# A hybrid decoder layer on one core: another order of the first products, the last tile's squares and root by blocks of 128 tokens, sums rounded in halves, one scaling by VectorE

## The chip, the core and the metric

The kernel runs on one core of a Trainium2 chip. The metric is the device time of one execution in microseconds (us); a run's time is that of its only core. Three runs of the kernel before took 1079.01, 1079.30 and 1079.93 us, median 1079.3. Each profile is of one more execution.

The core has five engines, each with its own queue of instructions, which it works through in order: TensorE (PE in the profile; its weight loads are PEld), VectorE (DVE), ScalarE (ACT), GpSimd (POOL) and SyncE (SP), which here only issues transfers. An instruction waits on semaphores for the instructions of other engines whose results or buffers it needs.

## What is computed

One inference layer over 576 tokens (a prompt of 512 and eight samples of 8), model width 1024:

```python
u = _rms(x) * g_pre_mix
proj = u @ w_in                       # split into the parts of two recurrences
...
mix = jnp.concatenate([y_ssd, h_ml], axis=-1) @ w_out
x = x + _rms(mix) * g_post_mix
u = _rms(x) * g_pre_x                 # cross-attention over 256 memory positions
...
o = jnp.einsum('bhlm,bmhd->blhd', pr, mem_v).reshape(bsz, length, X_WIDTH) @ w_xo
x = x + _rms(o) * g_post_x
u = _rms(x) * g_pre_ffn
f = (jax.nn.silu(u @ w_gate) * (u @ w_up)) @ w_down
x = x + _rms(f) * g_post_ffn
```

with `_rms(x) = x * rsqrt(mean(x * x) + eps)` per token. All in 32-bit floats; the kernel also returns the states of the recurrences and the memory's keys and values.

## The kernel before

**Products.** Every factor is kept as two tensors of a shorter format: a rounded part (`hi`: `whi`, `uh`, `hh`, `wdh`) and the remainder (`lo`: `wlo`, `ul`, `hl`, `wdl`). A cast, mostly by ScalarE, makes the rounded part; a subtraction, mostly by VectorE, makes the remainder (`split`, `split_w`). One product of a 128-row piece is then three matmuls into one PSUM bank: hi with hi, hi with lo, lo with hi (`gemm`, L201 to L212). The eight pieces of a 1024-long sum run one after the other. Features lie on the 128 partitions and tokens along the columns. The tokens go in two halves: 256 and 320 columns (`HALVES`) in the input projection and at the end, 288 and 288 (`EHALVES`) in between.

**Who sets the order.** Most of the program is handed to a planner, which orders the instructions of each engine by a simulated timeline, starting from the order of the program text; `tc.issue_after(i)` makes the instructions of its block follow `i` in the queue of their engine. The stretches under `tc.manual_schedule` (the middle of the kernel, and the end from L2302) run in an order written out by hand: `at_(p, fn)` puts a function at a place `p`, one unit being the products of one tile, and the sorted list is issued as it stands. Operations on one PSUM bank are kept in order as a whole.

**The start (L303 to L352).** `NWARM` products on zeros run on TensorE while the first transfers are under way. x arrives piece by piece (`xraw`, one piece of 128 features for each k; the first in two token halves), and two weight tiles (`raws`) arrive in four parts of two pieces each. ScalarE scales x into its rounded part (L333), VectorE makes the remainder (L334); the weights' parts are cast and subtracted behind them (L339, through L197 and L198; the very first cast is VectorE's, L330). TensorE takes, for each k and each of the two weight tiles, both token halves, three matmuls each (L350 to L352).

**The cross-attention's output (`xo`, from L1539).** Eight tiles of 128 features for the first 288 tokens. When a tile's products are done, ScalarE squares the bank (L270, L274 in `add_sq`) and scales it into `f` (L1560). For tiles 0 to 2 both are kept back until tile 3 begins (`kept_back`). Tile j takes a bank that tile j - 3 has given up, and its products are put behind `evx[j - 3]`, the last reading of that bank.

**The feed-forward part (from L1828).** `Pair` (gate and up projection) and `Down` (down projection) make two output tiles at once from seven products of combined factors instead of eight (`Seven`). For this, sums and differences of weights are made on VectorE (`sums`, into `sw`, the second half LB first, then LA) and split again (`parts2`: cast at L197, subtraction at L198). In `early` of a `Down` the order of the products is 0, 1, 3, 2; product 3 uses LB of the sum's parts, product 2 uses LA. Four `Down` groups run in each of two stages, beside the pairs.

**The last down projection (L2158 to L2173 and the list that follows).** It adds the last six of 22 pieces. Weights of tiles 0 to 4 go to `wdh` and `wdl` (cast and subtraction of 768 columns), those of tiles 5 to 7 to the usual buffers. The order for the second half of the tokens is tile 6, 7, 0, 1, 2, 3, 4, 5; the first three run their first four pieces before the last hidden values (`hh`, `hl`), which come from the last gate and up pair (`done`, L1935, then `put`), are there.

**The end (L2178 to L2304).** The 256 tokens of the first half go tile by tile (`half0`): the bank is added to `f2` (L2214), squared (L2217), scaled by the gain (L2219, for tile 7 by VectorE, L2221), and the squares are summed (L2224). For tile 7 the squares go straight into the sums over the features, products with ones (`root`, L2186), one column per block of 128 tokens. From these VectorE and ScalarE make the reciprocal root (L2190 to L2199; both blocks at once, as two columns). TensorE meanwhile turns `x` and `f2` into token rows (`x_rows`, `f_rows`); at the end VectorE adds root times rows to x for three of the four parts (`last`, L2270), ScalarE scales the fourth (`scaled`, L2280), VectorE adds it (`scaled_add`, L2283), and each part is stored.

Of the kernel before, what the change touches and what calls it, by code (L numbers as in the profile page):

```python
# [11 lines left out]
F32 = mybir.dt.float32  # L12
# [97 lines left out]
NWARM = 19  # L110
# [5 lines left out]
def build(nc, tc, ctx, I, O):  # L116
# [53 lines left out]
    loads, casts, accs = [], [], []  # L170
# [7 lines left out]
    def split_w(src, n=1024, cut=CUT, acc=False, pool=None, to=None, raw=None):  # L178
# [3 lines left out]
        if to:  # L182
            split(*to, raw[:, :n])
            return to
# [83 lines left out]
    def add_sq(pool, ssq, src, j, w=T, eng=None, t0=0, q=None):  # L268
        if j == 0:
            A.activation(ssq[:, t0:t0 + w], src, AF.Square)  # L270
# [45 lines left out]
    for k in range(KT):  # L316
# [11 lines left out]

        if k == 0:
            V.tensor_copy(wi[0][0][:, c], raws[0][:, c])  # L330
        for t0, n in ([(0, T)] if k else HALVES):
            ts_ = slice(t0, t0 + n)
            uhk = A.activation(uh[:, k, ts_], xraw[:, k, ts_], AF.Copy, scale=PAR("g_pre", k))  # L333
            ulk = V.scalar_tensor_tensor(ul[:, k, ts_], xraw[:, k, ts_], PAR("g_pre", k), uh[:, k, ts_].bitcast(F32),  # L334
                                         op0=ALU.mult, op1=ALU.subtract)
        if k % 2 == 0:
            for i in range(2):
                with tc.issue_after(uhk.ins), tc.issue_after(ulk.ins):
                    split(wi[i][0][:, c], wi[i][1][:, c], raws[i][:, c], cast=None if k or i else lambda *_: None)  # L339
# [5 lines left out]
    for k in range(KT):  # L345
        for (hi, lo), pss in zip(wi, ps0):
            wh, wl = hi[:, k * P:(k + 1) * P], lo[:, k * P:(k + 1) * P]
            for (t0, n), ps in zip(HALVES, pss):
                ah, al = U(k, t0, n), UL(k, t0, n)
                mm(ps, wh, ah, start=k == 0, stop=False)  # L350
                mm(ps, wh, al, start=False, stop=False)
                mm(ps, wl, ah, start=False, stop=k == KT - 1)  # L352
# [1186 lines left out]
    def xo(j, i, pool=None):  # L1539
# [11 lines left out]
        def step(k0, k1):  # L1551
# [5 lines left out]

            def out():
                add_sq(ph, ssq, ps, j if i == 0 else XO1.index(j), n, t0=t0)
                evx[at_e] = A.activation(f[:, j, t0:t0 + n], ps, AF.Copy, scale=PAR("g_postx", j))  # L1560
# [267 lines left out]
    class Seven:  # L1828
# [85 lines left out]
    class Pair(Seven):  # L1914
# [8 lines left out]
        def done(s, a, i, ps, more=None):  # L1923
# [11 lines left out]
            V.tensor_tensor(g, g, ps, op=ALU.mult)  # L1935
# [198 lines left out]
    class Plain:  # L2134
# [3 lines left out]
        def put(s, j, a, i, g):  # L2138
            split(*[t_[:, j % 8, E[i]] for t_ in s.b], g)
# [41 lines left out]
    def root(name, terms, chunks):  # L2181
# [5 lines left out]
        v, y, a, r = few[:] if n == 3 else [fp.tile([P, n], F32, name=name + k) for k in ("_v", "_y", "_a", "_r")]  # L2187
        w = fp.tile([P, n], F32, name=name + "_w")
        tail[name], tail["w", name] = (w, y, a, r), w
        V.tensor_scalar(v, ps[:, :n], 1.0 / 1024.0, EPS, op0=ALU.mult, op1=ALU.add)  # L2190
        A.activation(y, v, AF.Sqrt)
        V.reciprocal(tail["w", name], v)

    def root_end(name):
# [5 lines left out]
        tail[name] = r  # L2200
# [67 lines left out]
    def last(i):  # L2268
        o, rc = xt[i][0], tail["pf0"][:, parts[i][0]:parts[i][0] + 1]
# [8 lines left out]
    def scaled():  # L2278
        tail["s"] = sw[:, 0:512].rearrange("p (j k) -> p j k", j=4)
        A.activation(tail["s"], ft[3], AF.Copy, scale=tail["pf0"][:, parts[3][0]:parts[3][0] + 1])  # L2280

    def scaled_add():
        V.tensor_tensor(xt[3][0], xt[3][0], tail["s"], op=ALU.add)  # L2283
# [134 lines left out]
```

## Time and profile before

| | |
|---|---|
| median of three runs | 1079.3 us |
| the profiled execution | 1077.81 us |
| its span, first to last instruction | 1075.9 us |
| mean granted TensorE clock | 0.997 |
| busy: TensorE products, weight loads | 1066.2 us (99%), 1013.8 us (94%) |
| busy: VectorE, ScalarE, GpSimd | 751.8 us (70%), 607.6 us (56%), 231.7 us (22%) |
| matmuls | 8122 |
| last matmul ends, last VectorE operation ends, span ends | 1068.96, 1072.45, 1075.9 us |

Times in rows count from the first instruction. A matmul is pipelined: its recorded duration (0.28 to 0.31 us for 256 to 320 columns) is over twice the distance to the next one's start, so TensorE's share of busy time says little; the distance between starts says whether it waited.

### The profile page before, as it was taken

What the parts mean: (1) busy time and instruction counts of PE and PEld (TensorE: products, weight loads), DVE (VectorE), ACT (ScalarE), POOL (GpSimd) and SP (SyncE); (2) the same over time, 40 slices, a digit from 0 to 9 for tenths busy, and PEclk for the clock granted to TensorE, in tenths of its full rate; (3) what the DMA queues carried; (4) which work ended last, traced back from release to release, by engine and by line L of the source; (5) the groups of instructions that cost most, each with busy time, mean ns of one, the idle gap of its engine ahead of it and who ended that gap; (6) DMA issues with size and microseconds to landing.
All of it is one profiled execution on the core that took longest, in us unless ns stands there. A gap on an engine that the chain in (4) does not pass through costs nothing.

```text
span 1075.9 us, 20705 instructions
## 1 busy us (share of the span) xinstructions
PE 1066.2 (99%) x8122; PEld 1013.8 (94%) x8122; DVE 751.8 (70%) x1509; ACT 607.6 (56%) x1094; POOL 231.7 (22%) x305
## 2 busy tenths in 40 slices
PE   9999999999999999999999999999999999999997
PEld 8999887778999999999999989999999999999997
DVE  6897775758877775559655555766467887787556
ACT  7778522345654556556555445545566566656653
POOL 1454543213213111000154201100011111111000
PEclk9999999999999999999999999999999999999998
DMA  6785544435655349643468775743476687578532
GB/s 208 177 161 131 157 138 166 147 85 172 197 148 150 107 131 341 234 168 116 143 212 286 266 256 171 252 127 94 133 180 142 156 201 165 116 190 185 128 132 89
DMA packets 58966, 181.76 MB, mean 169 GB/s; under 512 B 6604, under 2 KB 12108, under 8 KB 58356
## 3 DMA queue, kind: packets, MB, share of 16 engines
q1 hardware_dynamic: 42884, 138.22, 38.4%
q0 software_dynamic: 15408, 41.43, 19.3%
q8 instruction: 64, 1.05, 0.4%
q10 hardware_dynamic: 576, 0.79, 0.2%
q14 instruction: 34, 0.28, 0.1%
HBM read 159.75 MB, written 20.65 MB: 168 GB/s over the span
## 4 chain that ended last, share of the span: by engine, by line
PE 95%; DVE 3%; ACT 1%; issue 1%; DMA 0%; SPq 0%; DVEq 0%; ACTq 0%
PE ps_in L208 6%; PE ps_in L211 6%; PE ps_in L209 6%; PE ps_v L854 5%; PE ps_o L211 3%; PE ps_g L1910 3%; PE ps_g L1909 3%; PE ps_o L209 3%; PE ps_g L1911 3%; PE ps_o L208 3%; PE ps_u L1910 3%; PE ps_u L1911 3%; PE ps_u L1909 3%; PE ps_dn L1909 2%; PE ps_dn L1910 2%; PE ps_dn L1911 2%
## 5 line engine op out<-in xcount | busy, mean ns | idle before, releaser
L208 PE MATMUL ps_in<-uh,whi 128*128 128x320 f32 (+1 forms) x544 | 161.7, 297 | 0.0
L211 PE MATMUL ps_in<-uh,wlo 128*128 128x320 f32 (+1 forms) x544 | 161.7, 298 | 0.0
L209 PE MATMUL ps_in<-ul,whi 128*128 128x320 f32 (+1 forms) x544 | 161.0, 296 | 0.0
L186 ACT CAST whi<-raw 128x1024 fp32r<-128x1024 f32 (+1 forms) x104 | 105.3, 1014 | 94.3 <-PE ps_in L209 27.7
L193 DVE TENSOR_TENSOR wlo<-raw,whi 128x1024 fp32r<-128x1024 f32 (+2 forms) x97 | 94.7, 978 | 59.6 <-ACT whi L186 58.7
L211 PEld LDWEIGHTS ps_in<-uh,wlo 128*128 128x128 f32 x544 | 102.1, 188 | 2.0 <-issue 1.3
L208 PEld LDWEIGHTS ps_in<-uh,whi 128*128 128x128 f32 x544 | 102.3, 188 | 1.7 <-issue 0.8
L209 PEld LDWEIGHTS ps_in<-ul,whi 128*128 128x128 f32 x544 | 102.3, 188 | 0.4
L191 POOL DMA_DIRECT2D wlo<-win x31 | 27.0, 872 | 78.0 <-ACT wlo L190 65.5
L1909 PE MATMUL ps_g<-b,whi 128*128 128x288 f32 x144 | 42.5, 295 | 0.0
L1910 PE MATMUL ps_g<-b,whi 128*128 128x288 f32 x144 | 42.4, 295 | 0.0
L1910 PE MATMUL ps_u<-b,whi 128*128 128x288 f32 x144 | 42.2, 294 | 0.0
L1909 PE MATMUL ps_u<-b,whi 128*128 128x288 f32 x144 | 42.2, 294 | 0.0
L1882 ACT CAST whi<-rawx 128x1024 fp32r<-128x1024 f32 (+1 forms) x26 | 25.7, 988 | 27.6 <-PE ps_dn L1910 13.7
L198 DVE TENSOR_TENSOR wlo<-sw,whi 128x1024 fp32r<-128x1024 f32 (+1 forms) x26 | 29.6, 1140 | 15.0 <-ACT whi L197 14.9
L208 PE MATMUL ps_xo<-qh,whi 128*128 128x288 f32 x128 | 38.4, 302 | 0.1
L209 PE MATMUL ps_xo<-ql,whi 128*128 128x288 f32 x128 | 37.7, 296 | 0.0
L211 PE MATMUL ps_o<-mixm_h,wlo 128*128 128x256 f32 (+1 forms) x128 | 37.7, 295 | 0.0
L209 PE MATMUL ps_o<-mixm_l,whi 128*128 128x256 f32 (+1 forms) x128 | 37.5, 293 | 0.0
L211 PE MATMUL ps_xq<-u2h,wlo 128*128 128x320 f32 (+1 forms) x128 | 37.5, 294 | 0.0
L211 PE MATMUL ps_o<-mixs_h,wlo 128*128 128x320 f32 (+1 forms) x128 | 37.4, 292 | 0.0
L209 PE MATMUL ps_xq<-u2l,whi 128*128 128x320 f32 (+1 forms) x128 | 37.4, 294 | 0.0
(770 smaller groups left out, 3842.2 us busy)
## 6 DMA issues: line engine op xcount, KB each, us to landing
raw<-win SPq DMA_DIRECT2D x35, 512.0 KB, 4.2
raw<-wout SPq DMA_DIRECT2D x17, 512.0 KB, 4.4
raw<-wxq SPq DMA_DIRECT2D x13, 512.0 KB, 3.9
raw<-wgate SPq DMA_DIRECT2D x13, 512.0 KB, 3.5
raw<-wup SPq DMA_DIRECT2D x13, 512.0 KB, 4.8
wlo<-win POOLq DMA_DIRECT2D x24, 256.0 KB, 5.1
kva<-vc SPq DMA_DIRECT2D x11, 512.0 KB, 6.6
raw<-wv SPq DMA_DIRECT2D x10, 512.0 KB, 4.3
```

Of the source, the lines that this page charges most:

```text
L186: casts.append(A.copy(hi[:, :n], raw[:, :n]))
L191: accs.append(G.dma_start(lo[:, a:b], src[:, a:b], accum_op=ALU.add))
L193: e.tensor_tensor(lo[:, a:b], raw[:, a:b], hi[:, a:b].bitcast(F32), op=ALU.subtract)
L198: (eng or V).tensor_tensor(lo, src, hi.bitcast(F32), op=ALU.subtract)
L208: mm(ps, wh, ah, start=i == 0, stop=False)
L209: mm(ps, wh, al, start=False, stop=False)
L211: m = mm(ps, tiles[order[c]][1], xh(order[c], t0, n), start=False, stop=c == len(tiles) - 1)
L854: mm(ps, a, b, skip_group_check=True, **kw)
L1882: A.copy(s.h3[:, s.all], s.r2[:, s.all])
L1909: mm(ps, wh, b[0][k], start=start and k == 0, stop=False, skip_group_check=True)
L1910: mm(ps, wh, b[1][k], start=False, stop=False, skip_group_check=True)
L1911: m = mm(ps, wl, b[0][k], start=False, stop=k == nk - 1, skip_group_check=True)
```

## The change

Four edits. The first piece's products are taken for both weight tiles in the first token half before the second half, with the operations that feed them in that order, and the warm-up has 17 products instead of 19. The cross-attention's tile 0 is scaled by VectorE when its products end. The down groups' sums are cast in two halves, LB first. At the end: tile 0's weight remainder in two pieces, some operations put behind others in their queues (tile 2's weights before tile 1's), tile 7's addition and squares by blocks of 128 tokens, block 0's root as before but for one column, block 1's root by five operations on GpSimd, and the last addition shared between GpSimd and VectorE.

```diff
-NWARM = 19
+NWARM = 17
...
         if to:
-            split(*to, raw[:, :n])
+            with tc.issue_after(after.ins) if after else ExitStack():
+                A.copy(to[0], raw[:, :n])
+            with tc.issue_after(behind.ins) if behind else ExitStack():
+                for a in range(0, n, piece or n):
+                    b = a + (piece or n)
+                    wlows.append(V.tensor_tensor(to[1][:, a:b], raw[:, a:b], to[0][:, a:b].bitcast(F32), op=ALU.subtract))
             return to
...
+        def x_parts(t0, n):
+            ts_ = slice(t0, t0 + n)
+            return (A.activation(uh[:, k, ts_], xraw[:, k, ts_], AF.Copy, scale=PAR("g_pre", k)),
+                    V.scalar_tensor_tensor(ul[:, k, ts_], xraw[:, k, ts_], PAR("g_pre", k), uh[:, k, ts_].bitcast(F32),
+                                           op0=ALU.mult, op1=ALU.subtract))
+
+        def w_parts(i):
+            hi, lo, raw = wi[i][0][:, c], wi[i][1][:, c], raws[i][:, c]
+            h = (A.copy if k or i else V.tensor_copy)(hi, raw)
+            return h, V.tensor_tensor(lo, raw, hi.bitcast(F32), op=ALU.subtract)
+
         if k == 0:
             V.tensor_copy(wi[0][0][:, c], raws[0][:, c])
-        for t0, n in ([(0, T)] if k else HALVES):
...
-        if k % 2 == 0:
-            for i in range(2):
+            x_parts(*HALVES[0])
+            V.tensor_tensor(wi[0][1][:, c], raws[0][:, c], wi[0][0][:, c].bitcast(F32), op=ALU.subtract)
+            h, l = w_parts(1)
+            with tc.issue_after(h.ins), tc.issue_after(l.ins):
+                uhk, ulk = x_parts(*HALVES[1])
+        else:
+            uhk, ulk = x_parts(0, T)
+            if k % 2 == 0:
                 with tc.issue_after(uhk.ins), tc.issue_after(ulk.ins):
-                    split(wi[i][0][:, c], wi[i][1][:, c], raws[i][:, c], cast=None if k or i else lambda *_: None)
+                    w_parts(0)
+                    w_parts(1)
...
     for k in range(KT):
-        for (hi, lo), pss in zip(wi, ps0):
+        for i, h in ((0, 0), (1, 0), (0, 1), (1, 1)) if k == 0 else ((0, 0), (0, 1), (1, 0), (1, 1)):
+            (hi, lo), (t0, n), ps = wi[i], HALVES[h], ps0[i][h]
             wh, wl = hi[:, k * P:(k + 1) * P], lo[:, k * P:(k + 1) * P]
-            for (t0, n), ps in zip(HALVES, pss):
-                ah, al = U(k, t0, n), UL(k, t0, n)
+            ah, al = U(k, t0, n), UL(k, t0, n)
+            with tc.issue_after(first.ins) if k == 0 and h else ExitStack():
                 mm(ps, wh, ah, start=k == 0, stop=False)
                 mm(ps, wh, al, start=False, stop=False)
-                mm(ps, wl, ah, start=False, stop=k == KT - 1)
+                m = mm(ps, wl, ah, start=False, stop=k == KT - 1)
+            if k == 0 and h == 0:
+                first = m
...
+            if (j, i) == (0, 0):
+                V.tensor_scalar(f[:, j, t0:t0 + n], ps, PAR("g_postx", j), None, op0=ALU.mult)
+
             def out():
-                add_sq(ph, ssq, ps, j if i == 0 else XO1.index(j), n, t0=t0)
-                evx[at_e] = A.activation(f[:, j, t0:t0 + n], ps, AF.Copy, scale=PAR("g_postx", j))
+                e = add_sq(ph, ssq, ps, j if i == 0 else XO1.index(j), n, t0=t0)
+                evx[at_e] = e if (j, i) == (0, 0) else A.activation(f[:, j, t0:t0 + n], ps, AF.Copy, scale=PAR("g_postx", j))
...
         def parts2(s):
...
-            split(s.h2[:, s.all], s.l2[:, s.all], sw[:, s.all])
+            for c in (s.LB, s.LA) if isinstance(s, Down) else [s.all]:
+                A.copy(s.h2[:, c], sw[:, c])
+            V.tensor_tensor(s.l2[:, s.all], sw[:, s.all], s.h2[:, s.all].bitcast(F32), op=ALU.subtract)
...
-            V.tensor_tensor(g, g, ps, op=ALU.mult)
+            s.product = V.tensor_tensor(g, g, ps, op=ALU.mult)
...
-            split(*[t_[:, j % 8, E[i]] for t_ in s.b], g)
+            s.cast = split(*[t_[:, j % 8, E[i]] for t_ in s.b], g)
...
         if j not in kept:
+            behind = {}
+            if j == 2:
+                behind[2] = last.product
+            if j == 1:
+                w_of(2)
+                behind[1] = wlows[-1]
...
-            kept[j] = split_w(src, 768, 768, raw=raw, to=None if j > 4 else (wdh[:, j, :], wdl[:, j, :]))
+            kept[j] = split_w(src, 768, 768, raw=raw, to=None if j > 4 else (wdh[:, j, :], wdl[:, j, :]),
+                              piece=384 if j == 0 else None, behind=behind.get(j), after=stores[-1].cast if j == 3 else None)
...
-        v, y, a, r = few[:] if n == 3 else [fp.tile([P, n], F32, name=name + k) for k in ("_v", "_y", "_a", "_r")]
+        v, y, a, r = [t_[:, 0:(3, 1)[n == 2]] for t_ in few]
...
-        V.tensor_scalar(v, ps[:, :n], 1.0 / 1024.0, EPS, op0=ALU.mult, op1=ALU.add)
+        V.tensor_scalar(v, ps[:, :v.shape[-1]], 1.0 / 1024.0, EPS, op0=ALU.mult, op1=ALU.add)
         A.activation(y, v, AF.Sqrt)
-        V.reciprocal(tail["w", name], v)
+        V.reciprocal(w, v)
+        if n == 2:
+            v, y, a, r = [fp.tile([P, 1], F32, name=name + k) for k in ("_v1", "_y1", "_a1", "_r1")]
+            V.tensor_scalar(v, ps[:, 1:2], 1.0 / 1024.0, EPS, op0=ALU.mult, op1=ALU.add)
+            G.tensor_tensor(y, v, C32("nhalf")[:, :1], op=ALU.pow)
+            G.tensor_tensor(a, y, y, op=ALU.mult)
+            G.tensor_tensor(a, a, v, op=ALU.mult)
+            G.tensor_scalar(a, a, -0.5, 1.5, op0=ALU.mult, op1=ALU.add)
+            G.tensor_tensor(r, a, y, op=ALU.mult)
+            tail["r", 1] = r
...
-        V.tensor_tensor(fj, fj, tail[j], op=ALU.add)
...
-        A.activation(squares[j] if j else ssqf[:, 0:256], fj, AF.Square)
+        o = squares[j] if j else ssqf[:, 0:256]
+        for c in [slice(0, 256)] if j < 7 else [slice(0, P), slice(P, 256)]:
+            V.tensor_tensor(fj[:, c], fj[:, c], tail[j][:, c], op=ALU.add)
+            A.activation(o[:, c], fj[:, c], AF.Square)
...
-        o, rc = xt[i][0], tail["pf0"][:, parts[i][0]:parts[i][0] + 1]
+        o, rc = xt[i][0], tail["r", parts[i][0]]
...
-        A.activation(tail["s"], ft[3], AF.Copy, scale=tail["pf0"][:, parts[3][0]:parts[3][0] + 1])
+        A.activation(tail["s"], ft[3], AF.Copy, scale=tail["r", 1])
...
-        V.tensor_tensor(xt[3][0], xt[3][0], tail["s"], op=ALU.add)
+        for e, j in ((G, slice(0, 2)), (V, slice(2, 4))):
+            e.tensor_tensor(xt[3][0][:, j], xt[3][0][:, j], tail["s"][:, j], op=ALU.add)
```

More of the change, by code (lines that the diff above doesn't have):

```diff
@@ L167, in build @@
     ident, ones = C32("ident"), C32("ones")
-    loads, casts, accs = [], [], []
+    loads, casts, accs, wlows = [], [], [], []
     def hi_lo(pool=None):
@@ L176, in hi_lo, with split_w @@
         return hi, (pool or wp).tile([P, 1024], F32R, name="wlo", tag="wlo", bufs=NWX if pool else 3)
-    def split_w(src, n=1024, cut=CUT, acc=False, pool=None, to=None, raw=None):
+    def split_w(src, n=1024, cut=CUT, acc=False, pool=None, to=None, raw=None, piece=None, behind=None, after=None):
         if raw is None:
@@ L269, in add_sq @@
         if j == 0:
-            A.activation(ssq[:, t0:t0 + w], src, AF.Square)
+            return A.activation(ssq[:, t0:t0 + w], src, AF.Square)
         else:
@@ L2199, in root_end @@
         V.scalar_tensor_tensor(r, r, 1.5, a, op0=ALU.add, op1=ALU.mult)
-        tail[name] = r
+        tail[name] = tail["r", 0] = r
     def root_rows1():
```

8 lines of the change are left out of this document (2 added, 6 removed).

## The prediction

> **What bounds the kernel now.** I read the chain of waits first, then TensorE's own waits, then the order of time around each place that the diff touches.
>
> ```profile
> PE 95%; DVE 3%; ACT 1%; issue 1%; DMA 0%; SPq 0%; DVEq 0%; ACTq 0%
> ...
> PE ps_warm L309 <- DVE wz L306: 1.1, 1, 1.1
> PE ps_in L350 <- ACT uh L333: 0.8, 1, 0.8
> PE ps_yi L682 <- DVE lm L675: 0.3, 1, 0.3
> PE ps_ct L589 <- ACT r L567: 0.2, 1, 0.2
> ```
>
> The first row is the chain that ended last, by engine: TensorE (PE) is 95% of it. The others are all the waits of TensorE that this view counts (who <- for whom: us, times, longest). No part of the change removes a counted product (two of the 19 warm-up products fall away, in front of the first stall), so a gain can only be a wait of TensorE that goes, or time before its first or after its last product. The view is short by some waits: a matmul's end is modelled and overlaps the next one, so a late start of under 0.15 us does not count as idle. Those are read from start to start in the order of time, below.
>
> **The start.** Order of time; columns are start, duration, engine, line, operation, and in brackets the idle time before it.
>
> ```profile
> 1.06 4.24 PE L309 MATMUL ps_warm<-wz 128*128 128x256 bf16 x19 [1.06 <-DVE wz L306]
> ...
> 5.25 0.28 PE L351 MATMUL ps_in<-ul,whi 128*128 128x256 f32 x1
> 6.37 0.68 PE L350 MATMUL ps_in<-uh,whi 128*128 128x320 f32 x2 [0.84 <-ACT uh L333]
> 9.56 0.69 PE L350 MATMUL ps_in<-uh,whi 128*128 128x256 f32 x4
> ...
> 5.75 0.56 ACT L333 ACTIVATE uh<-xraw,par 128x320 fp32r<-128x320 f32 x1 [1.81 <-DMA xraw<-xT]
> 8.68 0.70 ACT L197 CAST whi<-raw 128x256 fp32r<-128x256 f32 x2
> ```
>
> TensorE ran two products of the first piece, then stood from 5.25 to 6.37, because the second token half of x lands only for the 5.75 row. The change puts the six products of the first half (two weight tiles, three products each) ahead. What they need besides is made earlier: the second tile's rounding on ScalarE goes ahead of the 5.75 row into 1.81 us of idle time, and both tiles' remainders on VectorE ahead of the second half's. So four more 256-column products run inside the stall. Starts of 288-column products lie 0.13 us apart (rows of the next part), so 256 columns take 0.13 x 256/288 = 0.115 us, and four 0.46. The cap is the next weights: the piece that begins at 9.56 needs the two casts of the 8.68 row, the first of them done at about 9.07 and paced by transfers that the change doesn't move, so TensorE can begin it at 9.12 at best, 0.44 us earlier. I take **0.40**; the bounds are 0 (the new order only makes TensorE wait at 9.1 instead) and 0.46. The two warm-up products (4.24 us for 19, 0.21 us between starts) end 0.43 us earlier, all of it in front of the stall: worth nothing by itself, and nothing lost as long as the first product's weights, which were ready before the warm-up ended, stay so.
>
> **The first cross-attention output tile, one scaling by VectorE.**
>
> ```profile
> 634.21 0.41 ACT L270 ACTIVATE ssqxo<-ps_xo 128x288 f32<-128x288 f32 x1
> 634.51 0.49 ACT L1560 ACTIVATE f_xo<-ps_xo,par 128x288 f32<-128x288 f32 x1
> ...
> 634.50 0.30 PE L209 MATMUL ps_xo<-ql,whi 128*128 128x288 f32 x1
> 634.64 0.29 PE L211 MATMUL ps_xo<-qh,wlo 128*128 128x288 f32 x1
> 635.06 0.40 PE L208 MATMUL ps_xo<-qh,whi 128*128 128x288 f32 x1
> 635.29 0.30 PE L209 MATMUL ps_xo<-ql,whi 128*128 128x288 f32 x1
> ```
>
> Starts of 288-column products lie 0.13 us apart (0.14 in the first pair shown). From 634.64 to 635.06 it is 0.42, so 0.29 was waited, for the bank that L1560 releases at 635.00. The next interval, 0.23, is 0.10 over the normal one: a restart costs that too, since the weight load is no longer hidden. With the scaling on VectorE the bank is released by the square, at 634.62, ahead of 634.77 when TensorE wants it. The whole **0.39** goes. The new VectorE operation (about 0.45 us, an estimate from the 288-column addition at 1029.89 below) is issued when the tile's products end, several us earlier, off the chain; were it late, it could cost at most its own length there.
>
> **The down projection's sums rounded in halves.**
>
> ```profile
> 840.46 0.52 ACT L197 CAST u3h<-d 128x384 fp32r<-128x384 f32 x1
> 842.38 0.84 ACT L197 CAST whi<-sw 128x768 fp32r<-128x768 f32 x1 [0.65 <-PE ps_dn L1910]
> ...
> 842.92 0.29 PE L1911 MATMUL ps_dn<-te,wlo 128*128 128x288 f32 x1
> 843.27 0.41 PE L1909 MATMUL ps_dn<-hh,whi 128*128 128x288 f32 x1
> ...
> 942.90 0.29 PE L1911 MATMUL ps_dn<-te,wlo 128*128 128x288 f32 x1
> 943.24 0.41 PE L1909 MATMUL ps_dn<-hh,whi 128*128 128x288 f32 x1
> ```
>
> In both down stages TensorE waits once for the 768-column rounding: 0.35 and 0.34 from start to start, 0.21 over normal, and 0.10 of restart each. The product that waits is the one on the second half (LB), and that half is now rounded first: 384 columns take 0.52, so it is ready at 842.90 instead of 843.22, before 843.05 when TensorE is free. Both waits go: **0.62**. Two casts for one cost ScalarE about 0.2 us (2 x 0.52 against 0.84) in each of the eight groups; ScalarE is on 1% of the chain, so I count nothing, and 0 to -0.2 us per stage as the other bound, if the second half is then late.
>
> **The last down projection's weights.**
>
> ```profile
> 1027.78 0.96 DVE L198 TENSOR_TENSOR wdl<-raw,wdh 128x768 fp32r<-128x768 f32 x1 [0.41 <-ACT wdh L197]
> 1029.03 0.95 DVE L198 TENSOR_TENSOR wdl<-rawx,wdh 128x768 fp32r<-128x768 f32 x1
> 1029.89 0.45 DVE L1935 TENSOR_TENSOR gt<-gt,ct 128x288 f32<-128x288 f32 x1
> ...
> 1028.30 0.31 PE L208 MATMUL ps_dn<-hh,wdh 128*128 128x320 f32 x1
> 1028.45 0.31 PE L209 MATMUL ps_dn<-hl,wdh 128*128 128x320 f32 x1
> 1028.80 0.41 PE L211 MATMUL ps_dn<-hh,wdl 128*128 128x320 f32 x1
> ...
> 1030.50 0.30 PE L209 MATMUL ps_dn<-hl,wdh 128*128 128x320 f32 x1
> 1030.86 0.56 PE L208 MATMUL ps_dn<-hh,whi 128*128 128x320 f32 x2
> ```
>
> Two waits again. At 1028.80 (0.35 against 0.15) TensorE waits for tile 0's remainder, in one piece from 1027.78 to 1028.74; as two pieces of 384 the first is ready at about 1028.33, before 1028.60. At 1030.86 (0.36) it waits for the last hidden values, whose product (L1935, 1029.89) stood behind tile 1's remainder (1029.03). With that remainder put behind the product and behind tile 2's, the product can start 0.8 us earlier. With restarts that is 0.30 + 0.31 = **0.61**. What is late next: tile 1's remainder now ends near 1031.4 instead of 1029.97, and behind it on VectorE stand the hidden values' own remainders; TensorE has other tiles' first terms to run meanwhile, so I take the full 0.61 but keep 0 as the lower bound. On SyncE's queue the two loads change places; tile 5's load, which takes tile 1's buffer, goes about 1.4 us later with it, and that tile is the last in the order.
>
> **The tail.** TensorE's last sums, then the root, three scaled additions (L2270), the last addition (L2283) and the store; rows of POOL in groups of equal operation and shape (busy, mean ns).
>
> ```profile
> 1068.09 0.61 PE L2186 MATMUL ps_ss<-c,sq 128*128 128x1 f32 x4
> 1068.73 0.16 DVE L2190 TENSOR_SCALAR pf_v<-ps_ss 128x2 f32<-128x2 f32 x1 [0.76 <-PE ps_ss L2186]
> ...
> 1069.78 2.07 DVE L2270 SCALAR_TENSOR_TENSOR raw<-ps_ft,pf_r,raw 128x512 f32<-128x512 f32 x3
> 1069.84 0.69 ACT L2280 ACTIVATE sw<-ps_ft,pf_r 128x512 f32<-128x512 f32 x1 [0.72 <-DVE pf_r L2199]
> 1071.77 0.68 DVE L2283 TENSOR_TENSOR raw<-raw,sw 128x512 f32<-128x512 f32 x1
> ```
> ```profile
> L921 POOL TENSOR_TENSOR hn_y<-hn_v,c 128x1 f32<-128x1 f32 x2 | 1.1, 568 | 16.7 <-DVE hn_v L920 16.7
> ...
> L1000 POOL TENSOR_TENSOR qpad<-qk,vt 128x32 f32<-128x32 f32 x8 | 1.8, 254 | 0.0
> ...
> L485 POOL COPY cb<-cst 128x24 f32<-128x24 f32 x12 | 11.2, 937 | 0.0
> ...
> L198 POOL TENSOR_TENSOR mk<-mko,mk 128x256 fp32r<-128x256 f32 x6 | 4.4, 739 | 3.7 <-ACT mk L197 3.7
> ```
>
> By blocks, the first block's squares are summed while the second is squared, so two of the four sums (0.11 us each) come off: the root starts 0.22 earlier, at 1068.51. Block 0 keeps its root on VectorE, so L2270 starts at about 1069.56. Block 1's root goes to POOL as five operations: a power on one column (0.57, L921) and four small ones, of which tensor_scalar has no row on POOL. Their bounds are 0.25 (L1000) and 0.94 (L485, where other engines' work stretches them); I take 0.25, since few operations of any engine run beside them. Hand-overs come to 0.05 each (an estimate: VectorE's five dependent steps from 1068.73 to 1069.78 take 1.05, at 0.16 each 0.80), so 0.25 or 0.3 in all. VectorE makes block 1's mean square third in its row, at about 1068.9, and the root is there at 1068.9 + 0.57 + 1.0 + 0.3 = 1070.8. ScalarE's scaling then ends at 1071.5, POOL's half of the last addition (0.74, L198) at 1072.2, against 1072.45 for the 1071.77 row; VectorE's half is done by about 1071.9. I take **0.25**; the bounds are 0.5 (VectorE's half last) and a loss of 3.6, the second rival.
>
> [...]
>
> **The sum.** 0.40 + 0.39 + 0.62 + 0.61 + 0.25 = 2.27 us. The profiled execution took 1077.8 (span 1075.9), so it becomes 1075.5; the median of the runs, 1079.3, lies 1.5 above it and becomes **1077.0**. The places are tens of us apart, and between them the chain is TensorE's, so an earlier TensorE carries through.
>
> **The rivals.** First, the waits come back elsewhere: VectorE's or ScalarE's new order makes TensorE wait at the next piece (9.1 us, tile 1's remainder at 1031), the tail is even. The start and the last weights give nothing, and 0.39 + 0.62 remain with a tail of 0: 1078.3. For it: near 1031 VectorE's rows follow each other closely, and tile 1's remainder becomes the later one. Against it: the view of waits has nothing just behind any of these places.
>
> Second, on the other side: POOL's root decides the end. If the power takes three times L921 (1.7) and the small ones 0.94 each, the root is there at 1068.9 + 1.7 + 3.8 + 0.3 = 1074.7, the scaling ends at 1075.4 and the addition at 1076.1: 3.6 after today's 1072.45. Less 2.02 elsewhere, that is +1.6: 1080.9. It decides from a root later than about 1071.0, and the whole is slower than before from about 1073.0. For it: the mean of 937 ns. Against it: those copies stood beside heavy VectorE work.
>
> Third, more is gained: the order of the planned part is made anew from the first products on, and the waits of 0.3 and 0.2 in the second view go too, with 0.10 of restart each: 0.7 more, 1076.3. For it: both are waits for VectorE and ScalarE on an order that is planned; against it: nothing in the diff names them.
>
> That the change doesn't do what it says is no separate case: each edit moves instructions that the trace shows.
>
> **How the numbers follow.** About 0.2% (2.2 us, so below 1077.1 or above 1081.5) is what a measurement of this kernel can tell from no change. The forecast, 1077.0 with its own range of 1076.2 to 1077.9, has 0.48, of which 0.31 lies below 1077.1 and 0.17 above; the first rival 0.18, all within; the second 0.14, of which 0.08 over 1081.5, since its chain has no upper bound here, and 0.06 within; the third 0.20, all faster. That makes 0.31 + 0.20 = 0.51 faster, 0.17 + 0.18 + 0.06 = 0.41 within, 0.08 slower. The range is 1075.8 (half a microsecond under the third rival) to 1079.6 (above the first rival by 1.3, for a second one of half its size), which leaves out the second rival at its price.
>
> **What would show it.** Right: a first stall with six products before it and the 9.56 row at about 9.1; intervals of 0.13 to 0.15 at the five places; pf_v 0.2 earlier after the last sums; POOL's root within 2 us. Wrong: a new interval over 0.3 after 1031, ScalarE's last scaling waiting for POOL past 1071, or a later 9.56 row.

## The result, and the profile after

The changed kernel takes 1080.7 us (median of 22 runs, 1080.04 to 1082.77); the kernel before takes 1079.28 on the same chips (22 runs, 1077.98 to 1081.15). The ratio is 1.0014, 95% interval 1.0008 to 1.0020: 0.9 to 2.2 us slower. Forecast were 1077.0 and a range of 1075.8 to 1079.6, so both the number and its sign were wrong.

The profiled execution took 1080.15 us with a span of 1078.4, where before it was 1077.81 and 1075.9. The views that led the prediction, the chain by engine and TensorE's waits, look no worse than before:

```profile
PE 95%; DVE 3%; ACT 1%; DMA 1%; issue 0%; DVEq 0%; SPq 0%; ACTq 0%
...
PE ps_warm L314 <- DVE wz L311: 1.1, 1, 1.1
PE ps_in L369 <- ACT uh L336: 0.6, 1, 0.6
PE ps_ct L610 <- ACT r L588: 0.3, 1, 0.3
PE ps_dn L213 <- ACT wdh L184: 0.2, 1, 0.2
```

(Line numbers have moved: L208, L209, L211 are now L213, L214, L216; L2190 is L2223; L2283 is L2328.) The end of the kernel, in order of time, runs early too:

```profile
1067.69 0.16 DVE L2223 TENSOR_SCALAR pf_v<-ps_ss 128x1 f32<-128x1 f32 x1 [0.57 <-PE ps_ss L2219]
...
1068.19 0.57 POOL L2229 TENSOR_TENSOR pf_y<-pf_v,c 128x1 f32<-128x1 f32 x1 [43.89 <-DVE pf_v L2228]
...
1069.66 0.19 POOL L2233 TENSOR_TENSOR pf_r<-pf_a,pf_y 128x1 f32<-128x1 f32 x1
1069.89 0.69 ACT L2324 ACTIVATE sw<-ps_ft,pf_r 128x512 f32<-128x512 f32 x1 [1.81 <-POOL pf_r L2233]
...
1070.65 0.73 POOL L2328 TENSOR_TENSOR raw<-raw,sw 128x256 f32<-128x256 f32 x1 [0.80 <-ACT sw L2324]
1070.72 0.94 DVE L2328 TENSOR_TENSOR raw<-raw,sw 128x256 f32<-128x256 f32 x1
```

`pf_v` starts 1.04 us earlier than before (1068.73), and VectorE's last operation ends at 1071.66 where it ended at 1072.45. Yet the span ends 2.4 us later. What fills the time is in none of those views: the chain is followed back from the last operation that an engine executes (VectorE's, here), and the waits and the order of time leave out the DRAINs and semaphores that an engine's sequencer runs behind it. These closing instructions of the program have views of their own, here grouped by engine (columns: count; least, median and longest duration in ns; start of the first and of the last). First the changed kernel, then the kernel before:

```profile
L2458 POOLq EVENT_SEMAPHORE  x4: 17/17/17, 1077.6 to 1078.3; - x4
L2458 POOLq DRAIN  x3: 46/93/6974, 1070.6 to 1078.1; - x3
L2458 SPq DRAIN  x3: 7/7/7, 1074.2 to 1077.9; - x3
```
```profile
L2413 POOLq EVENT_SEMAPHORE  x4: 17/17/17, 1075.2 to 1075.8; - x4
L2413 POOLq DRAIN  x3: 46/102/6379, 1024.9 to 1075.7; - x3
L2413 SPq DRAIN  x3: 7/7/7, 1075.1 to 1075.4; - x3
```

Each engine ends with a DRAIN and then meets the others. SP reaches its own after the last store has landed: at 1074.2, 0.9 earlier than before. POOL's takes 6.97 us and runs from 1070.6 to 1077.6; only then come the semaphores, 0.7 us of them, and the end. Before, POOL's DRAIN was about as long (6.38), but it followed a memset and was over by 1031.2, far ahead of the end:

```profile
1024.88 0.15 POOL L1149 MEMSET ssqf<- 128x64 f32 x1 [14.81 <-DVE ct L1933]
```

The change gives POOL the last addition, and with it the drain 46 us later.

### The profile page after: what moved, and what is told of

The parts are those of the page before. It is cut to its first block, busy times and chain, and to the rows that moved or that the text cites. A ratio compares the mean times of both kernels' runs of the same rounds, so it can differ in the third digit from the quotient of the medians.

```text
span 1078.4 us, 20725 instructions
## 1 busy us (share of the span) xinstructions
PE 1065.7 (99%) x8120; PEld 1013.8 (94%) x8120; DVE 752.8 (70%) x1513; ACT 608.3 (56%) x1102; POOL 234.1 (22%) x311
## 3 DMA queue, kind: packets, MB, share of 16 engines
q8 instruction: 64, 1.05, 0.4%
## 4 chain that ended last, share of the span: by engine, by line
PE 95%; DVE 3%; ACT 1%; DMA 1%; issue 0%; DVEq 0%; SPq 0%; ACTq 0%
PE ps_in L213 6%; PE ps_in L216 6%; PE ps_in L214 6%; PE ps_v L875 5%; PE ps_o L216 3%; PE ps_g L1936 3%; PE ps_g L1935 3%; PE ps_o L214 3%; PE ps_g L1937 3%; PE ps_o L213 3%; PE ps_u L1936 3%; PE ps_u L1937 3%; PE ps_u L1935 3%; PE ps_dn L1935 2%; PE ps_dn L1937 2%; PE ps_dn L1936 2%
## 5 line engine op out<-in xcount | busy, mean ns | idle before, releaser
L216 PE MATMUL ps_in<-uh,wlo 128*128 128x320 f32 (+1 forms) x544 | 161.7, 298 | 0.0
L213 PE MATMUL ps_in<-uh,whi 128*128 128x320 f32 (+1 forms) x544 | 161.6, 297 | 0.0
L214 PE MATMUL ps_in<-ul,whi 128*128 128x320 f32 (+1 forms) x544 | 160.9, 296 | 0.0
L191 ACT CAST whi<-raw 128x1024 fp32r<-128x1024 f32 (+1 forms) x104 | 105.3, 1014 | 90.8 <-PE ps_in L214 27.3
L216 PEld LDWEIGHTS ps_in<-uh,wlo 128*128 128x128 f32 x544 | 102.2, 188 | 2.2 <-issue 1.3
L213 PEld LDWEIGHTS ps_in<-uh,whi 128*128 128x128 f32 x544 | 102.3, 188 | 1.6 <-issue 0.8
L214 PEld LDWEIGHTS ps_in<-ul,whi 128*128 128x128 f32 x544 | 102.3, 188 | 0.4
L1885 ACT CAST whi<-raw 128x1024 fp32r<-128x1024 f32 (+1 forms) x26 | 25.6, 984 | 22.7 <-PE ps_g L1936 11.8
L213 PE MATMUL ps_xo<-qh,whi 128*128 128x288 f32 x128 | 38.3, 301 | 0.0
L214 PE MATMUL ps_xo<-ql,whi 128*128 128x288 f32 x128 | 37.7, 296 | 0.0
L216 PE MATMUL ps_o<-mixm_h,wlo 128*128 128x256 f32 (+1 forms) x128 | 37.7, 295 | 0.0
L214 PE MATMUL ps_o<-mixm_l,whi 128*128 128x256 f32 (+1 forms) x128 | 37.5, 293 | 0.0
L216 PE MATMUL ps_xq<-u2h,wlo 128*128 128x320 f32 (+1 forms) x128 | 37.5, 293 | 0.0
L214 PE MATMUL ps_xq<-u2l,whi 128*128 128x320 f32 (+1 forms) x128 | 37.4, 294 | 0.0
```

The lines of the kernel that those rows point to most:

```text
L191: casts.append(A.copy(hi[:, :n], raw[:, :n]))
L213: mm(ps, wh, ah, start=i == 0, stop=False)
L216: m = mm(ps, tiles[order[c]][1], xh(order[c], t0, n), start=False, stop=c == len(tiles) - 1)
L1885: s.c1 = A.copy(s.h1[:, s.all], s.r1[:, s.all])
```

## The experiments

Theory A: POOL's drain ends some 6.2 us after POOL's last operation, whatever that is, and has set the end; without it the change gains. Rivals: B, the other edits lose the time; C, VectorE and POOL hold each other up in the halved addition.

**1. The changed kernel without POOL in its tail** (`k1_no_pool_tail`).

```diff
-        for e, j in ((G, slice(0, 2)), (V, slice(2, 4))):
-            e.tensor_tensor(xt[3][0][:, j], xt[3][0][:, j], tail["s"][:, j], op=ALU.add)
+        V.tensor_tensor(xt[3][0], xt[3][0], tail["s"], op=ALU.add)
...
-            G.tensor_tensor(y, v, C32("nhalf")[:, :1], op=ALU.pow)
```

with the root of both blocks as in the kernel before.

> The changed kernel with no GpSimd work in its tail: the root of both token blocks on VectorE and ScalarE as before, the last addition whole on VectorE; blocks kept. Theory A (the closing DRAIN of POOL, which ends 6.2 us after POOL's last instruction, sets the end of the changed kernel): POOL's last instruction is again near 1024 us, its drain is hidden, the span falls from 1078.4 to about 1075.0 and the time from 1080.7 to about 1077.4. Rival B (the edits at the start and at the last weights lose the time, the drain only fills a wait that is there anyway): span and time fall by 0.5 us at most. Rival C (VectorE and POOL hold each other up in the halved addition): about 0.3 us less, 1080.4.

**2. One column on POOL in the kernel before** (`k2_before_probe`).

```diff
         V.tensor_tensor(xt[3][0], xt[3][0], tail["s"], op=ALU.add)
+        G.tensor_copy(few[0][:, 0:1], tail["s"][:, 0, 0:1])
```

> The kernel before with one GpSimd copy of a single column added, which reads the last scaled tile and whose result nobody reads. Theory A: the copy runs at about 1070.6 to 1070.9 us, the drain ends 6.2 us later at about 1077.1, and 0.8 us after it the program: span 1077.8 in place of 1075.9, time 1081.2. Rival B or C: the copy is off every chain and the span stays at 1075.9, the time at 1079.3.

**3. Only the last addition taken from POOL** (`k3_root_only`): the first hunk of run 1 alone.

> The changed kernel with the last addition whole on VectorE; POOL keeps the root of the second block and so ends at 1069.86 us, 1.5 us earlier than in the changed kernel. Theory A: the drain ends at 1069.86 + 6.2 = 1076.1 and the program 0.8 later: span 1076.9, time 1079.2, half way between the changed kernel and the one without POOL's tail. Rival C (only the halved addition is at fault): as without POOL's tail, span 1075.0. Rival B: span 1078 or more.

**4. The whole tail of before in the changed kernel** (`k4_old_tail`).

```diff
-        for c in [slice(0, 256)] if j < 7 else [slice(0, P), slice(P, 256)]:
-            V.tensor_tensor(fj[:, c], fj[:, c], tail[j][:, c], op=ALU.add)
-            A.activation(o[:, c], fj[:, c], AF.Square)
+        V.tensor_tensor(fj, fj, tail[j], op=ALU.add)
+        A.activation(squares[j] if j else ssqf[:, 0:256], fj, AF.Square)
```

besides what run 1 undoes.

> The changed kernel with the whole tail of before (one piece of 256 tokens, one root on VectorE, one addition): only the four other edits are left. Theory A: they gain what TensorE is earlier at its last matmuls less the sums by blocks, about 0.8 us: span 1075.1, time 1078.5. Rival B: the four edits lose, time 1079.5 or more.

**5. The probe of run 2, ahead of the root** (`k7_early_probe`).

```diff
             V.tensor_scalar(sw[:, 512:768], fj, PAR("g_postffn", j), None, op0=ALU.mult)
+            G.tensor_copy(few[0][:, 0:1], squares[7][:, 0:1])
```

> The kernel before with the same one-column GpSimd copy as in the probe run, but reading the last tile's squares, so that it runs about 2 us earlier, some 6.4 us before the end of the last store's wait. Theory A: the drain ends 6.2 us after the copy, at the moment when the last store's landing is seen (1075.1 to 1075.2 us by the times of the kernel before), and costs 0 to 0.2 us: time 1078.8 to 1079.0. Rival (any GpSimd work in the tail costs, by being there): 2.3 us as in the probe run, 1081.1.

What these five gave. The third column is the distance from the start of `pf_v`, the first operation of the root, to the end of the span, which the other edits' gains and losses ahead of it don't enter; then the end of POOL's last operation and of its long DRAIN. A ratio is to runs of the kernel before that were made beside the run (median 1078.82 for runs 1 to 4, 1078.50 for run 5), not to the 1079.28 of the first row.

| run | median, ratio to before (95%) | `pf_v` to end | POOL's last | its DRAIN |
|---|---|---|---|---|
| before | 1079.28 | 7.22 | 1025.03 | 1031.24 |
| changed | 1080.7, 1.0014 (1.0008 to 1.0020) | 10.69 | 1071.38 | 1077.59 |
| 1, no POOL | 1077.12, 0.9988 (0.9980 to 0.9997) | 7.20 | 1025.89 | 1032.10 |
| 2, probe | 1081.15, 1.0021 (1.0012 to 1.0030) | 9.04 | 1073.41 | 1079.62 |
| 3, root only | 1080.01, 1.0010 (1.0001 to 1.0019) | 9.16 | 1070.97 | 1077.18 |
| 4, old tail | 1078.58, 0.9994 (0.9985 to 1.0003) | 7.20 | 1026.20 | 1032.41 |
| 5, early probe | 1079.56, 1.0007 (0.9998 to 1.0016) | 7.21 | 1069.25 | 1075.46 |

Run 1, without POOL at the end, has its closing instructions as the kernel before has them:

```profile
L2448 POOLq DRAIN  x3: 46/93/6381, 1025.7 to 1076.3; - x3
L2448 SPq DRAIN  x3: 7/7/7, 1075.7 to 1076.0; - x3
```

The two probes show the threshold: the late one (run 2; its copy starts 1.86 after `pf_v`), then the early one (run 5; 0.63 ahead of `pf_v`), each with POOL's copy in order of time and the closing instructions as above.

```profile
1073.22 0.19 POOL L2284 COPY pf_v<-sw 128x1 f32<-128x1 f32 x1 [45.56 <-ACT sw L2280]
...
L2414 POOLq DRAIN  x3: 46/93/6421, 1073.2 to 1080.1; - x3
L2414 SPq DRAIN  x3: 7/7/7, 1077.7 to 1079.9; - x3
```
```profile
1069.07 0.18 POOL L2222 COPY pf_v<-sq 128x1 f32<-128x1 f32 x1 [43.08 <-ACT sq L2217]
...
L2414 POOLq DRAIN  x3: 46/93/6419, 1069.0 to 1076.6; - x3
L2414 SPq DRAIN  x3: 7/7/7, 1076.1 to 1076.4; - x3
```

In run 2 the DRAIN ends at 1073.20 + 6.42 = 1079.6, 1.9 us after SP is done at 1077.7, and the distance to the end grows by 1.8. In run 5 it ends at 1075.46, 0.6 before SP at 1076.1, and the distance is that of before. The same copy of one column costs 1.8 us or nothing, by whether it comes 6.2 us ahead of the last store's landing. (The median of run 5 lies 1.1 over its reference, with an interval that includes no change; its trace shows nothing of it at the end.) Run 3 ends POOL's last operation 1.52 us nearer to `pf_v` than the changed kernel (2.17 after it, not 3.69), and its end comes 1.53 nearer. Run 1 gets 10.69 back to 7.20. Not all of that is the drain. VectorE's last operation ends 3.97 after `pf_v` starts in the changed kernel, 3.72 in run 1 and in the kernel before, 0.25 later. SP's first DRAIN, behind the last store, starts 6.54 after `pf_v` in the changed kernel and 6.38 in the other two, so 0.16 of the 3.47 that were lost (10.69 less 7.22) is work, and 3.31 the drain.

Against what was expected: the medians of runs 1, 2 and 4 came within 0.3 us of theory A's. Run 3 missed, with 1080.01 us for 1079.2 and a span of 1078.0 for 1076.9, which is what rival B was given there. Its trace puts the difference of the spans ahead of the tail: TensorE waits 1.1 us near 601 us, as the changed kernel's profile does not (see "What stays open"), and from `pf_v` on it takes 9.16 where the theory gives 9.2 (1076.9 less 1067.69). Run 5 was expected at 1078.8 to 1079.0.

So A stands, with its size. B falls: with the old tail (run 4) the other edits gain, if anything. C can be no more than VectorE's 0.25; run 6 looks at it.

**6. The last addition in halves, both on VectorE** (`k8_two_adds`; run 1 with this edit).

```diff
-        V.tensor_tensor(xt[3][0], xt[3][0], tail["s"], op=ALU.add)
+        for j in (slice(0, 2), slice(2, 4)):
+            V.tensor_tensor(xt[3][0][:, j], xt[3][0][:, j], tail["s"][:, j], op=ALU.add)
```

> As the run without POOL's tail, with the last addition as two halves of 128x256, both on VectorE. Theory (VectorE's half took 0.94 us in the changed kernel because POOL's half ran at the same time): 0.38 us each, half of the 0.68 for the whole and a fixed part. Rival (the half is that long by itself): about 0.9 us each.

One execution took 1077.25 us; in order of time:

```profile
1071.22 0.75 DVE L2319 TENSOR_TENSOR raw<-raw,sw 128x256 f32<-128x256 f32 x2
```

Two halves take 0.75 together, so one takes 0.38 (its own record says 0.42, and the two overlap); beside POOL's half it took 0.94. VectorE was held up, POOL (0.73) was not.

**7. The last weights: is it ScalarE's order?** The changed kernel has a new wait of TensorE just where the prediction looked for "what is late next". Order of time, changed kernel:

```profile
1027.05 1.03 DVE L188 TENSOR_TENSOR wdl<-raw,wdh 128x384 fp32r<-128x384 f32 x2 [0.41 <-ACT wdh L184]
...
1028.14 0.33 SPq L181 DMA_DIRECT2D raw<-wdown  x1
...
1031.09 0.84 ACT L184 CAST wdh<-raw 128x768 fp32r<-128x768 f32 x1 [0.94 <-DMA raw<-wdown]
...
1031.51 0.30 PE L213 MATMUL ps_dn<-hh,wdh 128*128 128x320 f32 x1
1031.98 0.42 PE L213 MATMUL ps_dn<-hh,wdh 128*128 128x320 f32 x1 [0.17 <-ACT wdh L184]
1032.24 0.31 PE L214 MATMUL ps_dn<-hl,wdh 128*128 128x320 f32 x1
```

0.47 and 0.25 from start to start where 0.15 is normal. I first blamed the rounding of tile 3, which the change puts behind the last hidden values (`k5_tile3_early`, run 1 with this edit).

```diff
-   piece=384 if j == 0 else None, behind=behind.get(j), after=stores[-1].cast if j == 3 else None)
+   piece=384 if j == 0 else None, behind=behind.get(j))
```

> As the run without POOL's tail, but the rounding of output tile 3's last weights is no longer put behind the last rounding of hidden values on ScalarE. Theory: that order makes TensorE's new wait near 1031.5 us (two intervals of 0.47 and 0.25 us where 0.15 is normal); without it both go to 0.15 and the time falls by 0.4 us, from 1077.1 to about 1076.7. Rival: the rounding of the hidden values comes later in its place and TensorE waits for it as in the kernel before (0.36 and 0.25): no change, 1077.1.

1078.06 us, ratio 0.9992 (0.9983 to 1.0001): no gain. The rival was right: TensorE now waited for the hidden values' rounding behind the product at 1030.43, 0.48 and 0.25 from start to start, and restarted once more at 1033.09.

```profile
1030.43 0.31 PE L216 MATMUL ps_dn<-hh,wdl 128*128 128x320 f32 x1
1030.90 0.56 PE L213 MATMUL ps_dn<-hh,whi 128*128 128x320 f32 x2 [0.17 <-ACT hh L202]
```

**8. Or the load of tile 4?** The rows above say more: ScalarE stands idle for 0.94 us ahead of the rounding at 1031.09, released by a transfer. Tile 4's is the fourth of these loads into two `raw` buffers, after those of tiles 6, 0 and 2; it is issued at 1028.14, when tile 0's remainder (1027.05 to 1028.08) frees one, and lands 2.9 us later. In `k9_tile4_load` (run 1 with this edit) it goes into a tile that is free.

```diff
-            raw = fp.tile([P, 1024], F32, name="rawx", tag="rawx", bufs=2) if j % 2 else None
+            raw = fp.tile([P, 1024], F32, name="rawx", tag="rawx", bufs=2) if j % 2 else sw if j == 4 else None
```

> As the run without POOL's tail, with the load of output tile 4's last weights put into a tile that is free from 1010 us on, so that it doesn't wait for tile 0's remainder to free its buffer at 1028.1 us. Theory: TensorE's wait near 1031.5 us (0.47 and 0.25 us, 0.43 over normal) is the chain buffer, load (2.9 us), rounding of tile 4; with the load early the rounding follows tile 3's on ScalarE at about 1030.2, the wait is gone, and the time falls by 0.4 us below the run without POOL's tail: about 1076.7, or a ratio of 0.9984. Rival (ScalarE's queue is what is late): an interval of 0.4 us or more stays near 1031 and the ratio stays at 0.9988.

1077.24 us, ratio 0.9985 (0.9976 to 0.9993), span 1074.7. Order of time:

```profile
1028.58 0.83 ACT L184 CAST wdh<-sw 128x768 fp32r<-128x768 f32 x1
...
1030.12 0.56 PE L213 MATMUL ps_dn<-hh,whi 128*128 128x320 f32 x2
1030.53 0.30 PE L213 MATMUL ps_dn<-hh,wdh 128*128 128x320 f32 x1
...
1031.69 0.31 PE L213 MATMUL ps_dn<-hh,wdh 128*128 128x320 f32 x1
1031.84 0.31 PE L214 MATMUL ps_dn<-hl,wdh 128*128 128x320 f32 x1
```

Tile 4 is rounded at 1028.58, ahead of the hidden values (behind tile 3, near 1030.2, was expected), and no interval is over 0.25: only one restart of 0.10 is left (1030.12 to 1030.53 for two). The trace settles the cause; the ratios of runs 1 and 8 (0.9988 and 0.9985) are too near each other to tell 0.3 us.

**9. The start.** The new order alone in the kernel before (`k6_start_alone`: the first hunks of the change, up to the products of the first piece, and 17 warm-up products).

> The kernel before with the new order of the first piece and the 17 warm-up products alone. By the prediction the piece that began at 9.56 us begins 0.40 us earlier and the time is 1078.4 us where before takes 1078.8. By the traces so far (3.19 us from the first product on x's second half to that piece in the kernel before, 3.08 and 2.99 in two runs with the new order) the gain is 0.1 to 0.2 us, below what the times can tell: 1078.7. Rival (the new order costs, since fewer warm-up products leave TensorE slow at its first products): 1079.2 or more.

1078.73 us, ratio 0.9998 (0.9989 to 1.0007): nothing that the times can tell. The trace has 3.07 us from the first product on x's second half to the third piece, against 3.19.

**10 and 11.** The start of before in the kernel of run 8 (`k10_old_start`), and 19 warm-up products there with the new order kept (`k11_warm19`, whose edit against run 8 is this).

```diff
-NWARM = 17
+NWARM = 19
```

> The best kernel so far (no POOL tail, tile 4's load early: ratio 0.9985) with the start of the kernel before: old order of the first piece, 19 warm-up products. In three profiles with the old order the time from the first product on x's second half to the third piece is 3.19, 3.60 and 4.73 us, and grows with the stall ahead of it (0.84, 0.98, 1.77); in eight with the new order it is 2.94 to 3.08. Theory (the new order is worth 0.1 to 1.7 us by how late x lands, 0.8 on the mean of the three): 3.2 us or more here, and a ratio of 0.9992. Rival (the new order is worth the predicted 0.40 or less in the median): ratio 0.9985 to 0.9989.

> The best kernel so far with 19 warm-up products in place of 17 and the new order kept. By the prediction the warm-up lies in front of a stall and its length is worth nothing: ratio 0.9985, 3.0 us from the first product on x's second half to the third piece. Rival (the two products keep TensorE fast across the stall, and it is the warm-up and not the order that counts): under 2.8 us, and a ratio of 0.9983 or less; or the first piece starts later and the stall grows shorter by the same.

Run 10: 1078.41 us, ratio 0.9988 (0.9978 to 0.9999), and 3.19 us after a stall of 1.60. The stall's length does not set the pace after it, and against run 8 (0.9985) the theory that the new order is worth 0.8 is not borne out. Run 11: 1076.96 us over 7 runs, ratio 0.9974 (0.9963 to 0.9984), 2.98 us: the pace is as the prediction has it, the ratio as the rival asked. Its interval overlaps that of run 8, so the warm-up's length stays worth nothing that is shown. Runs 10 and 11 were made beside the same runs of the kernel before and differ in the order alone: 1.45 us by the medians, with intervals that just overlap. What the order is worth in a typical execution stays open. The intervals of runs 1, 8, 10 and 11 all lie below 1.

## Why the prediction was wrong

**The step that failed** is the tail, "I take **0.25**": it followed the root, the scaling and the halves of the addition up to the last operation, compared its end with 1072.45, and took the end of work for the end of the program. Each stage there has a price in a row, but "POOL's half of the last addition" also moves POOL's last instruction, and the program cannot end before POOL's drain. The rows were in the trace of before, 6.38 us long and hidden. In place of +0.25, the tail lost 10.69 - 7.22 = 3.47 us from `pf_v` on, 0.16 by work and 3.31 by the drain; the blocks won 0.13 ahead of `pf_v`. The work itself was followed well: POOL's half was forecast to end 3.69 after `pf_v` (1072.2 less 1068.51) and did so (1071.38 less 1067.69), by small errors that cancel; VectorE's half, forecast to end 0.3 ahead of POOL's, ended 0.28 behind it, held up.

Of the text's signs of being wrong, two came, a new interval over 0.3 after 1031 (0.47) and a later 9.56 row (9.71); ScalarE's last scaling did not wait past 1071 (it starts at 1069.89). None of the signs looks at the end of the program.

**The second rival** named the right engine, and its 1080.9 is close to the 1080.7 measured, but by another mechanism. It needed a root later than 1071.0 and priced one at 1074.7; the root was there at 1069.66 + 0.19 = 1069.85, the power taking 0.57 and the small operations 0.19 or 0.20 each. POOL was as fast as forecast, and still decided the end.

**The rest of the sum** was right in direction and, but for one term, too large. `pf_v` starts 1.04 us earlier; the terms that lie ahead of it:

| term | forecast | measured |
|---|---|---|
| start | 0.40 | 0.12 (run 9), 0.11 (changed), from the first product on x's second half to the third piece |
| one scaling by VectorE | 0.39 | 0.39 |
| down sums in halves | 0.62 | 0.35 |
| last weights | 0.61 | 0.18 |
| sums by blocks | 0.22 | 0.13 |

The last four make 1.05, and the 1.04 of `pf_v` is theirs: at 634.64 the two profiles are level (the row stands in both, below). The start's gain is not in it, since ahead of 634 the two executions differ in other things too. The changed one begins the second half of x 0.26 later (6.63 for 6.37) and the third piece 0.15 later; and it lacks the wait of 0.3 for `lm`, which the third rival named. That one is not the change's gain: no profile but that of before has it, and the start of before is also in runs 2, 5 and 10. The 0.18 is the 0.61 of before less the 0.43 of the new wait (0.47 and 0.25 less twice 0.146); the 0.13 is the time from the start of the last down product to `pf_v`, 1.89 us with the old sums and 1.76 by blocks.

*Scaling:* exact. After the product at 634.64 the next starts at 634.77, with VectorE's row off the chain:

```profile
633.39 0.52 DVE L1580 TENSOR_SCALAR f_xo<-ps_xo,par 128x288 f32<-128x288 f32 x1 [1.36 <-PE ps_xo L216]
...
634.64 0.29 PE L216 MATMUL ps_xo<-qh,wlo 128*128 128x288 f32 x1
634.77 0.30 PE L213 MATMUL ps_xo<-qh,whi 128*128 128x288 f32 x1
634.91 0.29 PE L214 MATMUL ps_xo<-ql,whi 128*128 128x288 f32 x1
```

*Down sums:* the wait for the second half went as forecast, and the first half became late, the case that the text held as its other bound.

```profile
841.99 0.93 ACT L1894 CAST whi<-sw 128x384 fp32r<-128x384 f32 x2 [0.65 <-PE ps_dn L1936]
...
842.66 0.29 PE L1935 MATMUL ps_dn<-hh,whi 128*128 128x288 f32 x1
842.79 0.29 PE L1936 MATMUL ps_dn<-hl,whi 128*128 128x288 f32 x1
842.97 0.40 PE L1935 MATMUL ps_dn<-hh,whi 128*128 128x288 f32 x1
843.21 0.29 PE L1936 MATMUL ps_dn<-hl,whi 128*128 128x288 f32 x1
```

The product at 842.66 no longer waits, but two products later, at 842.97, TensorE wants the half that is ready at 841.99 + 0.93 = 842.92. It waits 0.05, and a wait of 0.05 costs the whole restart of 0.11 (842.97 to 843.21 is 0.24). Each of the two stages had 0.33 over normal and has 0.16, a gain of 0.17 or 0.18 where 0.31 was forecast.

*Last weights:* the two waits named went. Tile 4's load, which was a buffer behind in the kernel before too, came up as a wait of 0.43; "TensorE has other tiles' first terms to run meanwhile" was read without that load, of which the text says nothing.

*Start:* the six products ran ahead of the stall as said. Of the four that this moves (0.46), most is given back behind it, since the second half now meets its own remainder late. Changed kernel:

```profile
6.61 0.55 DVE L337 SCALAR_TENSOR_TENSOR ul<-xraw,par,uh 128x320 fp32r<-128x320 f32 x1 [1.31 <-ACT uh L336]
6.63 0.56 PE L369 MATMUL ps_in<-uh,whi 128*128 128x320 f32 x2 [0.64 <-ACT uh L336]
7.21 0.41 PE L370 MATMUL ps_in<-ul,whi 128*128 128x320 f32 x1
7.47 0.31 PE L371 MATMUL ps_in<-uh,wlo 128*128 128x320 f32 x1
```

The third product of that half waits for `ul` until 7.21, with restarts around it (0.58 for the first two products and 0.26 for the third, where 0.15 each is normal). In the old order first-half products stood there and covered the remainder.

**What stays open.** By the two profiles the change costs 2.4 us, by the medians 1.4 (0.9 to 2.2), by the lowest runs of each (1077.98 and 1080.04) 2.1. The profiled execution before, 1077.81, is under all of its 22 runs. One profile does not stand for the median, since executions differ by whole waits. TensorE's waits in run 1, then in run 3:

```profile
PE ps_o L213 <- ACT f_mix L1146: 0.8, 1, 0.8
```
```profile
PE ps_os L1465 <- ACT kva L1490: 1.1, 1, 1.1
```

The first, near 423 us, stands behind a load (`prel` from `wup`) to which the chain of run 1 gives 7.65 us; runs 2 and 11 have it too, with 0.6. The second, near 601 us, is also in runs 1 and 4. TensorE runs the same order of products in runs 1 and 3 as in the changed kernel, whose profile has neither wait, nor has that of before. How often each comes is not on record. A loss by the old order of the start that is larger in a typical run than in the profile of before would be another reason: run 9 and run 10 against run 8 did not show it, run 10 against run 11 leaves room for it.

## What to carry to other kernels

Before moving work to an engine at the end of a kernel, ask when that engine's last instruction was until now, and read the closing instructions of every engine: an engine with a long drain may be free for work in the middle and dear at the end. A cover found for one late operand must be followed to the next operand that TensorE wants, back through buffers and loads; of the two gains named here where the next one was close behind, 0.18 of 0.61 and 0.35 of 0.62 were left. A wait of 0.05 us of TensorE cost a restart of 0.11 besides, so a wait must go wholly to be worth its price.

## What the runs showed of the hardware

POOL's closing DRAIN ended 6.21 us after the end of POOL's last operation in each of the seven kernels of the table (1025.03 to 1031.24, 1071.38 to 1077.59, 1069.25 to 1075.46), after a memset, a copy of one column, a product of one column (run 3) and an addition alike. From SP's last wait, the end of the program takes 0.8 us where POOL is done (1075.1 to 1075.9 in the kernel before).

Of two halves of one addition that started 0.07 us apart, POOL's took 0.73 us, as subtractions of that size on POOL do in the kernel before (0.74), and VectorE's 0.94 in place of 0.42. The Trainium skill's page "SBUF — State Buffer", section "Who interferes with whom", says that a VectorE instruction with two SBUF inputs contends with a GpSimd instruction that reads SBUF, and that the order of issue decides which of them blocks. POOL started first (1070.65 against 1070.72), so the trace agrees; no run has the other order.

In run 2 TensorE was granted half its clock just after the first stall; the kernel before had the full one. Columns: window, length, busy time of five engines, granted clock, DMA share, GB/s; the kernel before, then run 2.

```profile
8.00:10.00 2.00, 2.00 (x17) 2.00 (x17) 1.49 (x4) 2.00 (x4) 0.00 (x0) 1.00 1.06 390
```
```profile
8.00:10.00 2.00, 2.00 (x10) 2.00 (x9) 1.79 (x4) 1.85 (x4) 0.00 (x0) 0.50 1.02 366
```

Ten products instead of 17 in those 2 us, and 4.73 us from the first product on x's second half to the third piece instead of 3.19. The stall ahead of it was 1.77 us; run 10 had one of 1.60 and kept the full clock. Run 4 was granted half of it from 84 to 86 us (0.50, ten products), so the first stall is not the only place.
